# A two-layer hybrid transformer kernel: stores issued from GpSimd, attention loads for two heads at once, and other weave ratios

## The chip, the cores and the metric

The kernel runs on one core of one Trainium2 chip. A core has five engines that work side by side, each with its own instruction stream: PE (TensorE, matrix products), DVE (VectorE), ACT (ScalarE), POOL (GpSimd) and SP (SyncE, which here only issues transfers). Transfers between the device's memory and the core's on-chip memory (DMA) are issued by SP, ACT or POOL; an issue stands in the engine's stream like any other instruction, and what comes behind it waits for it. The metric is the device time of one execution, in microseconds.

## The reference

The input is 2048 latent tokens of width 1024, with 256 context tokens in front (18 tiles of 128 tokens in all). Layer 0 is "even", layer 1 is "odd". Cut to what matters:

```python
# each layer: h = rms_norm(x) * (1 + scale) + shift, for latent and context; x = x + gate * y
# layer 0 (even)
u = h @ w_in                       # q_lat, kv_lat, k_rope, za, gq, gk, gv, gate ranks, zb
q, k, v = mla_heads(q_lat, kv_lat, k_rope)       # 8 heads, 96-wide q and k, 64-wide v
a = softmax(q @ k.T * 96 ** -0.5) @ v            # every latent token sees all 2304
b = gla_bidirectional(gq, gk, gv, gates)         # 4 heads, gated scan in chunks of 64, both ways
y = concat([a * silu(za), rms_norm(b) * silu(zb)]) @ w_out
# layer 1 (odd)
q, k, v, z = split(h @ w_in, 4)                  # 16 heads, 64 wide; q and k normalised
s = q @ k_window.T / 8 + rpb                     # window of 8 rows x 16 columns on a 64-wide grid
p = softmax(concat([s, q @ k_ctx.T / 8]))
y = ((p @ concat([v_window, v_ctx])) * silu(z)) @ w_out
```

All is float32. The kernel gets products of that accuracy from three matmuls of split numbers: a factor is written as a high part and a low part, and high times high, high times low and low times high are summed.

## The kernel before

The layers run in stages, one after the other, and each leaves its results in device memory:

- `even_latent`: layer 0's latent projections, which give the queries `QT`, the keys `KT` and the values `Vn` (with high and low parts).
- `even_rest` (L540): the other projections of layer 0. Cells (tile t, column group j) of 24 matmuls each (8 steps of 3) give za (`zaT`) and the inputs of the gated scan (`Un`, in pieces of 352 or 512 columns). Woven between them are `maxes()`: for each of the 8 heads the largest score of every query row, 82 matmuls `mx` and as many reductions on DVE (L592), then one transpose (L597) and a store of the negated row `mr` into row 96 of `QT`. Attention later gets the shift of its exponential from that row.
- `even_mix` (L916): `even_attention` (L784), interleaved with the gated scan `gla` (L605), then `project` (L975) with the output weights. While it projects, `ahead()` prepares layer 1: it splits weights and prepares two token tiles (`prep`: load `x`, normalise, transpose at L299, store `H`).
- `odd_qk` (L1012): layer 1's queries and keys (`Q`, `K`), and two first cells of the values.
- `odd_vz` (L1088): the rest of the values (`V1c` for context, `V1` for latent tokens) and the gate z. Its `maxes()` goes over 16 heads: products of queries and keys, a table `mtab` that POOL makes for each head with two additions (L1134, L1135), maxima on DVE (L1151, L1162), a transpose (L1169), and four small stores `M`.
- `odd_attention` (L1181): pairs of heads j = 0 to 7, scores at L1244 and L1245, then the output projection.

In attention, scores `st` are three matmuls per key tile `kt` and head (L889, L890, L892), then an exponential on ACT, the product with the values (`av`, L865) and running sums on DVE and POOL. `keys`, `low`, `values` and `queries` issue the loads, all from SP: `akh` (high key parts with the row 96), `akl` (low parts), `av` (values), `aqh` and `aql` (queries). The first pair of heads loads in two halves; later pairs are loaded ahead while the pair before runs.

`weave(main, side, ratio, lag)` (L128) sets how two streams mix: after each step of `main` it adds `ratio` to a count and takes as many steps of `side` as the count has whole numbers. `lag` keeps `main` from being issued ahead of the side step that lies that many steps back. What is left of `side` comes at the end.

The order of instructions on each engine is fixed when the program is built: a scheduler places them by its own estimate of their times, and `issue_after` forbids it to place one before another. Waits between engines go over semaphores. Transfers issued by SP and ACT share eight DMA semaphores in turn, and a transfer waits until the one before it on its semaphore has landed; those issued by POOL have eight others. Buffers in on-chip memory come from pools; `bufs` is the number of buffers of a name, and memory of a closed pool is reused as soon as its last users are done.

Stores leave from these queues: `zaT`, `Un` of 352 columns, the maxima's rows, `V1c`, `V1` and `M` from ACT; `Un` of 512 columns from SP (two from POOL); `Q`, `K`, `QT`, `KT` from SP. Raw weights (`wraw`, L343) go through two buffers, and are split on ACT and DVE (L346).

The central lines of the weave and of its uses are

```python
due += ratio
while due >= 1:
    due -= 1
    r = next(side, None)
...
self.weave(gemms, maxes(), 1.0, 30)     # even_rest
self.weave(gemms, maxes(), 0.5, 15)     # odd_vz
```

## Time and profile before

| | us |
|---|---|
| median of 3 runs | 3861.09 (3860.72 to 3863.76) |
| the profiled execution | 3867.9 |
| its span, first to last instruction | 3866.1 |
| PE busy in it | 3670.2 |
| DVE busy | 2347.1 |
| ACT busy | 1475.4 |
| POOL busy | 1269.1 |

The mean clock granted to PE in this execution is 0.972 of full speed. Stages by the times of their first and last instructions: `even_rest` some 566 to 1124, scores of the even attention from 1124 to 2062 with the scan between them, `odd_vz` some 2715 to 3191, `odd_attention` from there on.

How rows are read. A timeline row gives start, duration, engine, line, operation, output and inputs with their sizes (partitions x elements), and in brackets the idle time of the engine before it with what ended that; a `q` behind an engine's name (SPq) is its issuing of transfers. A row of waits gives total, number and longest. A row of windows gives the stretch, its length, then for PE, PEld (loading of weights), DVE, ACT and POOL the busy time with the number of instructions, and last the granted clock, the share of the DMA engines' time and the GB/s. A row of a line gives durations in ns (least, median, largest) and first and last start.

### The profile page before, as it was taken

Reading aid. Unit: us, or ns where it says so; the run is one execution under the profiler, and the core shown is the slowest. Engines: PE = TensorE matmul, PEld = TensorE weight load, DVE = VectorE, ACT = ScalarE, POOL = GpSimd, SP = SyncE. Lnnn points to the kernel's source line nnn. Section 1 sums busy time; section 2 is a strip of 40 time slices with the busy share of each in tenths; the row PEclk is TensorE's granted clock in tenths of the full one; section 3 lists DMA queues with packets and bytes.
Section 4 is the critical chain, followed back from the end, with each engine's and each line's share of the span. In section 5 each row is a group of like instructions: output and inputs, shape, how many; then the busy total and the mean of one; then the engine's idle time right before and its main releaser. Section 6 shows DMA issues by size and latency. Waiting matters only on the chain. (4 is left out here: it accounts for less than half of the span.)

```text
span 3866.1 us, 52721 instructions
## 1 busy us (share of the span) xinstructions
PE 3670.2 (95%) x18388; PEld 2767.7 (72%) x18388; DVE 2347.1 (61%) x4699; ACT 1475.4 (38%) x2928; POOL 1269.1 (33%) x1356
## 2 busy tenths in 40 slices
PE   7999979999979999999999999999999997889899
PEld 4999878888866666555556788888788874555577
DVE  4677757888855556586654344444677765667632
ACT  3555541111115555545553123333322225656610
POOL 0334320000004444454543223333222215667622
PEclk8999989999989999999999999999999998999999
DMA  6455553222241232323514544445544468797553
GB/s 236 138 152 148 155 166 90 75 85 77 69 130 59 75 99 75 90 86 111 148 57 136 164 142 126 131 128 154 176 135 132 138 136 207 182 204 183 146 150 114
DMA packets 387175, 503.09 MB, mean 130 GB/s; under 512 B 30691, under 2 KB 265611, under 8 KB 380424
## 3 DMA queue, kind: packets, MB, share of 16 engines
q1 hardware_dynamic: 339174, 447.83, 41.1%
q10 hardware_dynamic: 47576, 51.37, 4.2%
q8 instruction: 146, 2.39, 0.3%
q14 instruction: 119, 0.97, 0.1%
q0 software_dynamic: 160, 0.52, 0.0%
HBM read 329.68 MB, written 169.93 MB: 129 GB/s over the span
## 5 line engine op out<-in xcount | busy, mean ns | idle before, releaser
L106 ACT ACTIVATE apt<-st 128x512 f32<-128x512 f32 (+1 forms) x592 | 346.1, 592 | 340.7 <-PE st L892 306.3
L592 DVE TENSOR_REDUCE mm<-mx 128x1 f32<-128x512 f32 (+1 forms) x656 | 393.2, 628 | 102.8 <-PE mx L591 95.5
L880 DVE TENSOR_TENSOR acc<-acc,apt 128x512 f32<-128x512 f32 x288 | 253.9, 903 | 174.9 <-ACT apt L106 173.4
L865 PE MATMUL av<-apt,av 128*64 128x512 f32 (+1 forms) x1184 | 306.9, 605 | 0.0
L880 POOL TENSOR_TENSOR acc<-acc,apt 128x512 f32<-128x512 f32 x160 | 216.4, 1366 | 238.6 <-ACT apt L106 237.9
L1291 POOL TENSOR_TENSOR oacc<-oacc,opt 128x341 f32<-128x341 f32 (+6 forms) x336 | 237.4, 738 | 116.5 <-ACT opt L106 92.9
L889 PE MATMUL st<-aqh,akh 97*128 97x512 f32 (+1 forms) x592 | 264.0, 446 | 11.1 <-ACT apt L106 5.8
L591 PE MATMUL mx<-mk,mq 96*128 96x512 f32 (+1 forms) x656 | 239.7, 375 | 9.4 <-DMA mq<-QT 8.5
L1162 DVE CUSTOM_DVE_ANT_1 mx<-mx,mtab 128x225 f32<-128x225 f32 (+13 forms) x576 | 180.8, 341 | 103.5 <-PE mx L1156 56.3
L890 PE MATMUL st<-aql,akh 96*128 96x512 f32 (+1 forms) x592 | 236.0, 399 | 1.2 <-DMA aql<-QT 1.2
L892 PE MATMUL st<-aqh,akl 96*128 96x512 f32 (+1 forms) x592 | 234.7, 397 | 0.0
L889 PEld LDWEIGHTS st<-aqh,akh 97*128 97x128 f32 x592 | 112.7, 191 | 137.9 <-issue 76.5
L106 ACT ACTIVATE u<-gm 128x352 f32<-128x352 f32 (+1 forms) x140 | 69.0, 498 | 357.8 <-PE gm L125 283.8
L1351 DVE TENSOR_TENSOR opt<-st,tab 128x64 f32<-128x64 f32 (+10 forms) x576 | 145.1, 313 | 73.1 <-PE st L1245 51.3
L570 POOL DMA_DIRECT2D Un<-u x2 | 1.4, 676 | 565.6 <-DVE u L559 565.6
L998 POOL TENSOR_TENSOR px<-py,px 128x512 f32<-128x512 f32 x68 | 91.2, 1343 | 283.9 <-DVE py L997 277.2
L865 PEld LDWEIGHTS av<-apt,av 128*64 128x64 f32 x1184 | 76.9, 137 | 143.3 <-issue 139.9
L997 DVE TENSOR_TENSOR py<-pj,gate 128x512 f32<-128x512 f32 x68 | 46.9, 690 | 218.0 <-PE pj L116 217.9
L1134 POOL TENSOR_TENSOR mtab<-mtab,maskq 128x1798 f32<-128x1798 f32 x16 | 51.4, 3212 | 325.0 <-DMA mtab<-rpb_q 251.1
L106 ACT ACTIVATE opt<-opt 128x465 f32<-128x465 f32 (+7 forms) x256 | 122.6, 497 | 53.6 <-DVE opt L1351 47.2
L1244 PE MATMUL st<-q,kt 128*128 128x480 f32 (+5 forms) x256 | 101.0, 406 | 39.1 <-ACT opt L106 20.9
L591 PEld LDWEIGHTS mx<-mk,mq 96*128 96x128 f32 x656 | 122.1, 189 | 22.2 <-issue 8.8
(419 smaller groups left out, 10301.7 us busy)
## 6 DMA issues: line engine op xcount, KB each, us to landing
q<-Q SPq DMA_DIRECT2D x48, 512.0 KB
kb<-K SPq DMA_DIRECT2D x192, 128.0 KB
H<-x ACTq DMA_DIRECT2D x36, 512.0 KB
pr<-RT SPq DMA_DIRECT2D x34, 512.0 KB
adaw<-ada_w SPq DMA_DIRECT2D x64, 256.0 KB
x<-H SPq DMA_DIRECT2D x32, 512.0 KB
wraw<-w_od SPq DMA_DIRECT2D x64, 256.0 KB
mtab<-rpb_q SPq DMA_DIRECT2D x16, 899.0 KB
```

The lines of the kernel that those rows point to most:

```text
L106: return self.nc.scalar.activation(out, in_, func, **kw)
L591: mm = nc.tensor.matmul(ps[:, :w], q[:A_QK, (t % 6) * P : (t % 6) * P + P], k[:A_QK, k0 : k0 + w], start=True, stop=True)
L592: nc.vector.tensor_reduce(out=m[:, t, n : n + 1], in_=ps[:, :w], axis=AX.X, op=ALU.max)
L865: nc.tensor.matmul(av[i * 64 : i * 64 + 64, :w], V[:, kt, i * 64 : i * 64 + 64], pts[i][:, :w], start=n == 0, stop=n == len(kts) - 1)
L880: eng.tensor_tensor(out=acc[i][e][:, :w], in0=a[:, :w], in1=pts[i][:, :w], op=ALU.add)
L889: nc.tensor.matmul(ps[:, :w], kh[: A_QK + 1, ks], qh[: A_QK + 1, :w], start=True, stop=False)
L890: nc.tensor.matmul(ps[:, :w], kh[:A_QK, ks], ql[:A_QK, :w], start=False, stop=False)
L892: mm = nc.tensor.matmul(ps[:, :w], kl[:A_QK, kq : kq + P], qh[:A_QK, :w], start=False, stop=True)
L1162: nc.vector.tensor_tensor_reduce(out=s, in0=s, in1=tb[:, ri : ri + rn, ci : ci + cn], scale=1.0, scalar=-3e38, op0=ALU.add, op1=ALU.max, a ...
L1244: nc.tensor.matmul(ps, k1, q1, start=True, stop=False)
L1291: eng.tensor_tensor(out=a, in0=a, in1=pts[i][:, a0 - r0 : a1 - r0, :], op=ALU.add)
L1351: nc.vector.tensor_tensor(out=pt[:, d[0], d[1]], in0=ps[:, d[0], d[1]], in1=tabs[i][:, ri : ri + rn, ci : ci + cn], op=ALU.add)
```

## The change

The diff does these things:

- `weave` gets `head`: a negative start of the count, so that the side stream begins `head` steps later. Once the side stream is at its end, each step that it would have taken is counted in `over`, and the bound on the main stream moves on by that many side steps.
- `even_rest` weaves with ratio 1.06 and head 20 in place of 1.0; `odd_vz` with 0.57 in place of 0.5.
- The stores `zaT`, all of `Un`, the maxima's rows into `QT`, `V1c`, `V1` and `M` are issued by POOL. In the built program ACT has 208 transfers fewer, SP has 110 instructions fewer, and POOL has 224 transfers more; DVE's and PE's instructions are the same in number.
- `even_attention` loads keys, low parts and queries of both heads of a pair in one transfer each, into tiles with a head dimension. The first pair comes in pieces of 384, 768 and 1152 columns. The second block's queries are issued after the first pieces, before the others. The next pair's keys are loaded in block 2 (both heads) and its values in block 4; before, it was one head each in blocks 2 and 3.
- `ahead()` yields once more behind each `prep`, so that the next one comes a project tile later.
- Raw weights of layer 1 have three buffers in place of two.
- `odd_attention` loads the first pair's values after the tables.

```diff
@@ -125,15 +125,17 @@
             yield
-    def weave(self, main, side, ratio, lag):
-        due, done = 0.0, []
+    def weave(self, main, side, ratio, lag, head=0):
+        due, done, over = -float(head * ratio), [], 0.0
         while True:
             with ExitStack() as es:
-                if len(done) > lag:
-                    es.enter_context(self.tc.issue_after(done[-lag - 1].ins))
+                n = len(done) - lag - 1 + int(over)
+                if n >= 0:
+                    es.enter_context(self.tc.issue_after(done[min(n, len(done) - 1)].ins))
                 if next(main, self) is self:
@@ -141,7 +143,9 @@
                 r = next(side, None)
-                if r is not None:
+                if r is None:
+                    over += 1
+                else:
                     done.append(r)
@@ -278,9 +282,9 @@
             nc.sync.dma_start(self.gates[l, :, (b - 4) * 512 : (b - 4) * 512 + 512], row[:])
-    def prep_pool(self, es, name, side, bufs):
+    def prep_pool(self, es, name, side, bufs, wbufs):
         self.prp = self.pool(es, name, bufs=2, side=side, reuse_waits="tile")
-        self.hbufs = bufs
+        self.hbufs, self.wbufs = bufs, wbufs
     def prep(self, l, t, src, pp, tag):
@@ -331,7 +335,7 @@
         nc = self.nc
-        sp, bufs, width = stage or (self.prp, 2, cols)
+        sp, bufs, width = stage or (self.prp, self.wbufs, cols)
         if place is None:
@@ -565,11 +569,11 @@
                     self.act(z[:], pt[:])
-                    nc.scalar.dma_start(self.zaT[:, :, t * P : t * P + P].rearrange("j p t -> p j t"), z[:])
+                    nc.gpsimd.dma_start(self.zaT[:, :, t * P : t * P + P].rearrange("j p t -> p j t"), z[:])
                 elif j == 1:
-                    (nc.gpsimd if t < 2 else nc.sync).dma_start(self.Un[t, :, 1056:], u[:])
+                    nc.gpsimd.dma_start(self.Un[t, :, 1056:], u[:])
                 else:
-                    nc.scalar.dma_start(self.Un[t, :, (j - 2) * 352 : (j - 1) * 352], u[:, :352])
+                    nc.gpsimd.dma_start(self.Un[t, :, (j - 2) * 352 : (j - 1) * 352], u[:, :352])
             cells = self.cells(list(range(NT))[::-1], (2, 3, 4, 0, 1), lambda t, j: j not in (2, 3) or t < NT - 2)
@@ -597,10 +601,10 @@
                     self.act(r[:NT], ps[:NT, :P], AF.Copy, scale=-1.0)
-                    nc.scalar.dma_start(self.QT[h, 0, A_QK].rearrange("(t p) -> t p", p=P), r[:NT].bitcast(F32))
+                    nc.gpsimd.dma_start(self.QT[h, 0, A_QK].rearrange("(t p) -> t p", p=P), r[:NT].bitcast(F32))
                     yield mm
-            self.weave(gemms, maxes(), 1.0, 30)
+            self.weave(gemms, maxes(), 1.06, 30, 20)
     def gla(self, gp, gs, g1, gd, pp, tag):
@@ -785,75 +789,70 @@
         half = T // 2
-        def keys(j, i):
-            kh = self.tl(ap, [P, T], f"akh{i}", F32R, bufs=2)
-            src = self.KT[2 * j + i, 0]
-            cuts = (0, half, T) if j == 0 else (0, T)
+        firsts = (0, 3 * P, half)
+        def keys(j):
+            kh = self.tl(ap, [P, 2, T], "akh", F32R, bufs=2)
+            cuts = firsts + (T,) if j == 0 else (0, T)
             for a, b in zip(cuts, cuts[1:]):
-                nc.sync.dma_start(kh[:A_QK, a:b].bitcast(F32), src[:A_QK, a:b])
-                nc.sync.dma_start(kh[A_QK : A_QK + 1, a:b].bitcast(F32), src[A_QK : A_QK + 1, a:b])
-                if b < T:
-                    yield kh
-            yield kh
+                nc.sync.dma_start(kh[:A_QK, :, a:b].bitcast(F32), self.KT[2 * j : 2 * j + 2, 0, :A_QK, a:b].rearrange("h p t -> p h t"))
+                nc.sync.dma_start(kh[A_QK : A_QK + 1, :, a:b].bitcast(F32),
+                                  self.KT[2 * j : 2 * j + 2, 0, A_QK : A_QK + 1, a:b].rearrange("h p t -> p h t"))
+                yield kh
         def values(j):
             V = self.tl(ap, [P, NT, P], "av", bufs=2)
-            cuts = (0, NT // 2, NT) if j == 0 else (0, NT)
+            cuts = [c // P for c in firsts + (T,)] if j == 0 else (0, NT)
             for a, b in zip(cuts, cuts[1:]):
...
         def low(j, p):
-            kl = [self.tl(ap, [P, half], f"akl{p}{i}", F32R, bufs=1) for i in range(2)]
-            for i in range(2):
-                nc.sync.dma_start(kl[i][:A_QK].bitcast(F32), self.KT[2 * j + i, 1, :A_QK, p * half : (p + 1) * half])
-            return kl
+            kl = self.tl(ap, [P, 2, half], f"akl{p}", F32R, bufs=1)
+            cuts = firsts if j + p == 0 else (0, half)
+            for a, b in zip(cuts, cuts[1:]):
+                nc.sync.dma_start(kl[:A_QK, :, a:b].bitcast(F32),
+                                  self.KT[2 * j : 2 * j + 2, 1, :A_QK, p * half + a : p * half + b].rearrange("h p t -> p h t"))
+                yield kl
         def queries(j, q0, w):
-            Q = []
-            for i, h in enumerate((2 * j, 2 * j + 1)):
-                qh = self.tl(ap, [P, 512], f"aqh{i}", F32R, bufs=2)
-                ql = self.tl(ap, [P, 512], f"aql{i}", F32R, bufs=2)
-                nc.sync.dma_start(qh[:A_QK, :w].bitcast(F32), self.QT[h, 0, :A_QK, q0 : q0 + w])
-                nc.sync.dma_start(qh[A_QK : A_QK + 1, :w].bitcast(F32), self.QT[h, 0, A_QK : A_QK + 1, q0 : q0 + w])
-                last = nc.sync.dma_start(ql[:A_QK, :w].bitcast(F32), self.QT[h, 1, :A_QK, q0 : q0 + w])
-                Q.append((qh, ql))
-            return Q, last
-        nextK, nextV = [None, None], None
+            q = self.tl(ap, [P, 4, 512], "aq", F32R, bufs=2)
+            nc.sync.dma_start(q[:A_QK, :, :w].bitcast(F32), self.QT[2 * j : 2 * j + 2, :, :A_QK, q0 : q0 + w].rearrange("h z p t -> p (h z) t"))
+            return q, nc.sync.dma_start(q[A_QK : A_QK + 1, 0::2, :w].bitcast(F32),
+                                        self.QT[2 * j : 2 * j + 2, 0, A_QK : A_QK + 1, q0 : q0 + w].rearrange("h p t -> p h t"))
+        nextK = nextV = None
+        early = {}
         for j in range(4):
-            rest = []
             if j == 0:
-                Q, _ = queries(0, 0, CTX)
-                gens = [keys(0, i) for i in range(2)] + [values(0)]
-                K = [next(g) for g in gens[:2]]
-                L = [low(0, 0)]
-                V = next(gens[2])
-                rest = gens
+                early[0], _ = queries(0, 0, CTX)
+                gens = [keys(0), low(0, 0), values(0)]
+                K, L0, V = [next(g) for g in gens]
+                early[1], _ = queries(0, CTX, 512)
+                for g in gens:
+                    next(g)
+                next(gens[0])
+                L = [L0, next(low(0, 1))]
+                next(gens[2])
             else:
-                K = list(nextK)
-                V = nextV
-                L = [low(j, 0), low(j, 1)]
+                K, V = nextK, nextV
+                L = [next(low(j, p)) for p in range(2)]
             for nb, (q0, w, kts) in enumerate(blocks):
-                if j or nb:
+                if j == 0 and nb in early:
+                    Q = early.pop(nb)
+                else:
                     Q, last = queries(j, q0, w)
...
                 nc.sync.dma_start(zt[:, :w], self.zaT[j, :, q0 : q0 + w])
-                if j < 3 and nb > 1:
+                if j < 3 and nb in (2, 4):
                     with self.tc.issue_after(last.ins):
-                        if nb < 4:
-                            nextK[nb - 2], = keys(j + 1, nb - 2)
+                        if nb == 2:
+                            nextK, = keys(j + 1)
                         else:
...
                 yield
-                if rest:
-                    for g in rest[:2]:
-                        next(g)
-                    L.append(low(0, 1))
-                    next(rest[2])
-                    rest = []
                 av = self.tl(pp, [P, 512], "av", bufs=2)
@@ -883,13 +882,12 @@
                     for i in range(2):
-                        kh = K[i]
-                        qh, ql = Q[i]
+                        qh, ql = Q[:, 2 * i, :], Q[:, 2 * i + 1, :]
                         ps = self.tl(pp, [P, 512], "st", bufs=3)
-                        nc.tensor.matmul(ps[:, :w], kh[: A_QK + 1, ks], qh[: A_QK + 1, :w], start=True, stop=False)
-                        nc.tensor.matmul(ps[:, :w], kh[:A_QK, ks], ql[:A_QK, :w], start=False, stop=False)
-                        kl, kq = L[kt // (NT // 2)][i], (kt % (NT // 2)) * P
-                        mm = nc.tensor.matmul(ps[:, :w], kl[:A_QK, kq : kq + P], qh[:A_QK, :w], start=False, stop=True)
+                        nc.tensor.matmul(ps[:, :w], K[: A_QK + 1, i, ks], qh[: A_QK + 1, :w], start=True, stop=False)
+                        nc.tensor.matmul(ps[:, :w], K[:A_QK, i, ks], ql[:A_QK, :w], start=False, stop=False)
+                        kl, kq = L[kt // (NT // 2)], (kt % (NT // 2)) * P
+                        mm = nc.tensor.matmul(ps[:, :w], kl[:A_QK, i, kq : kq + P], qh[:A_QK, :w], start=False, stop=True)
                         pt = self.tl(ap, [P, 512], "apt", bufs=8)
@@ -950,7 +948,7 @@
             pp = self.pool(es, "woP", bufs=2, space=PSUM, reuse_waits="tile")
-            self.prep_pool(e1, "prp1", "left", 2)
+            self.prep_pool(e1, "prp1", "left", 2, 3)
             ws = [self.pool(e1, "owS", side="left", reuse_waits="tile")]
@@ -958,6 +956,7 @@
                     hT[t] = self.prep(1, t, self.x1, pp, ("pj", 4))
+                    yield
                     yield
@@ -1079,11 +1078,11 @@
         if t < NCT:
-            self.nc.scalar.dma_start(self.V1c[:, t, c], v[:])
+            self.nc.gpsimd.dma_start(self.V1c[:, t, c], v[:])
             return
...
         for r in range(2):
-            self.nc.scalar.dma_start(self.V1[a + r, g * 64 : g * 64 + 64, c], v[r * 64 : r * 64 + 64])
+            self.nc.gpsimd.dma_start(self.V1[a + r, g * 64 : g * 64 + 64, c], v[r * 64 : r * 64 + 64])
     def odd_vz(self, ws, win, hT):
@@ -1170,12 +1169,12 @@
                     for g in range(4):
-                        nc.scalar.dma_start(self.M1[h, g * 512 : g * 512 + 512].rearrange("(a c b) -> c a b", a=8, c=4),
+                        nc.gpsimd.dma_start(self.M1[h, g * 512 : g * 512 + 512].rearrange("(a c b) -> c a b", a=8, c=4),
                                             r[4 * g : 4 * g + 4].rearrange("c (a b) -> c a b", a=8).bitcast(F32))
...
             gemms = self.stream(cells, hT, cell, lambda t: self.reload(1, t))
-            self.weave(gemms, maxes(), 0.5, 15)
+            self.weave(gemms, maxes(), 0.57, 15)
     def odd_attention(self, ld, right, wout):
@@ -1249,15 +1248,18 @@
                 kc = keys(j, 0, CTX, "kc")
-                V = values(j)
                 if j == 0:
...
                         pass
+                else:
+                    V = values(j)
                 if mk is None:
...
                 tabs = [table(2 * j + i, i) for i in range(2)]
+                if j == 0:
+                    V = values(j)
                 O, acc = {}, {}
@@ -1388,7 +1390,7 @@
         with ExitStack() as e0:
-            self.prep_pool(e0, "prp0", "right", 2)
+            self.prep_pool(e0, "prp0", "right", 2, 2)
             ws = self.pool(e0, "ewS", side="left", reuse_waits="tile")
```

## The prediction

> **What bounds the kernel now.** I read the summary of the engines first, then what PE's idle time waited for, then the span in short windows, and last the timeline around each hole.
>
> ```profile
> span 3866.1 us, 52721 instructions
> PE 3670.2 (95%) x18388; PEld 2767.7 (72%) x18388; DVE 2347.1 (61%) x4699; ACT 1475.4 (38%) x2928; POOL 1269.1 (33%) x1356
> ...
> PE st L1244 <- ACT opt L106: 23.8, 19, 3.5
> ...
> PE gm L123 <- ACT onat L106: 7.0, 1, 7.0
> ```
>
> PE, the matmul engine, is busy 95% of the span, so only 195.9 us (3866.1 − 3670.2) are idle. The changed program, as built, holds the same matmuls, only in another order. The time can therefore fall only by PE's idle time and by the slow clock that follows it; no engine's saving counts as such. The largest entry (L1244 on ACT, 19 short waits inside layer 1's attention) belongs to work that the change leaves alone. The rest of what it can reach sits in seams between stages. Two are large: even projections to even attention, and odd projections to odd attention.
>
> ```profile
> 1110.00:1160.00 50.00, 29.53 (x104) 19.92 (x103) 16.17 (x30) 12.12 (x24) 4.88 (x10) 0.69 0.77 204
> 3180.00:3220.00 40.00, 18.29 (x53) 11.02 (x53) 15.86 (x54) 8.52 (x16) 7.11 (x3) 0.58 1.01 210
> ```
>
> In each row the first number after the length is PE's busy time; the last three are granted clock, DMA share and GB/s. PE idles 20.5 us (50 − 29.53) from 1110 to 1160 and 21.7 us from 3180 to 3220, and what runs there runs at a mean clock of 0.69 and 0.58. Those two holes are most of what this change can win.
>
> **Step B, the first row maximum of the even weave (edit: head=20).**
>
> ```profile
> 566.33 0.32 PE L125 MATMUL gm<-W2h,hlo 128*128 128x352 f32 x1
> 566.49 0.32 PE L123 MATMUL gm<-W2h,hhi 128*128 128x352 f32 x1
> ...
> 581.62 2.04 PE L591 MATMUL mx<-mk,mq 96*128 96x256 f32 x5 [8.53 <-DMA mq<-QT]
> ```
>
> PE reaches its first maximum after 43 projection matmuls and waits 8.53 us for the queries' load. In the changed program 63 such matmuls stand ahead of it, 20 more: 352-column ones are 0.16 us apart (566.33 to 566.49), 512-column ones 0.24 (1116.62 to 1116.86, below). 15 of them are of the wide kind, so 5 × 0.16 + 15 × 0.24 = 4.4 us of the wait is filled. The load itself is no earlier: it waits for stores that the change doesn't touch. Bounds 3.2 us (all narrow) to 6; I take 4.
>
> **Step C, into the even attention (lead and ratio 1.06, two heads per load, pieces, stores off ACT).**
>
> ```profile
> 1116.62 0.40 PE L123 MATMUL gm<-wr1h,hhi 128*128 128x512 f32 x1
> 1116.86 0.39 PE L124 MATMUL gm<-wr1l,hhi 128*128 128x512 f32 x1
> 1117.32 2.88 PE L591 MATMUL mx<-mk,mq 96*128 96x512 f32 x8
> ...
> 1124.21 0.38 PE L597 MATMUL mx<-ident,mc 128*18 128x128 f32 x1 [2.52 <-DVE mc L595]
> ...
> 1136.27 0.76 PE L889 MATMUL st<-aqh,akh 97*128 97x512 f32 x1 [5.24 <-DMA aqh<-QT]
> 1147.37 0.45 PE L641 MATMUL gl<-ident,gu 128*96 128x128 f32 x1 [10.34 <-POOL gu L640]
> 1149.03 0.79 PE L890 MATMUL st<-aql,akh 96*128 96x512 f32 x1 [1.22 <-DMA aql<-QT]
> ...
> 1105.30 0.30 SPq L795 DMA_DIRECT2D akh<-KT  x1
> 1113.37 0.22 SPq L796 DMA_DIRECT2D akh<-KT  x1
> 1131.56 0.30 SPq L819 DMA_DIRECT2D aqh<-QT  x1
> 1136.69 1.24 SPq L636 DMA_DIRECT2D gu<-Un  x2
> ```
>
> The last projection is issued before 1117.32; then come left-over maxima, a few scores, and holes of 5.24 and 10.34 us. Even flow returns at 1149.03. In these 31.7 us (timeline rows not all shown) stand 10 maxima, 25 score, value and sum matmuls and two transposes, some 6 us at full clock, so 26 are lost. Three things make the loss. First, the maxima end after the projections: in the changed program their last transpose stands 39 matmuls (9 us) before the last projection. Second, SP is late: between its loads at 1105.30 and 1113.37 it stood 8.1 us. In the program that is a wait on a DMA semaphore which SP's loads share with ACT's stores; with the stores on POOL it goes, and the loads wait only for the buffers of the projections whose weights lie there: the queries' and first keys' buffers are free 42 us or more before the end, the first values' 12 to 15 us before. Third, the second block's queries (1131.56) and the gating inputs (1136.69) stand at the end of SP's queue. Now these queries are issued ahead of the later pieces, and the first gating transpose stands some 17 us of score and value work into the attention instead of behind one score matmul. What is late next: that transpose again (its load is still behind some 5 MB of keys and values; the 204 GB/s of this window move them in 25 us, from 12 to 15 us before the projections' end, so 0 to 4 us of wait remain), and the keys' third piece. The saving is 26 less 2 for the gating wait and 3 for a slower clock at the start: 21; I take 20. Bounds: 10, if the transfers set the pace (rival 1), and 26.
>
> **Step E, project and prepare (one more yield).**
>
> ```profile
> 2180.91 0.32 SPq L290 DMA_DIRECT2D x<-x  x1
> 2188.40 1.97 PE L299 MATMUL pj<-ident,x 128*128 128x128 f32 x8 [4.87 <-DVE x L296]
> 2190.59 0.63 PE L115 MATMUL pj<-gu,prh 128*128 128x512 f32 x1
> 2191.01 0.63 PE L116 MATMUL pj<-gu,prl 128*128 128x512 f32 x1
> ```
>
> PE's transposes of the second tile wait 4.87 us for x, whose load leaves at 2180.91, when the single buffer is free. With the extra yield one project tile of 48 matmuls (11 us at 0.24) stands before them, more than the wait. The matmuls after it took 0.42 us each (2190.59 to 2191.01) instead of 0.24, for some 3 us: 1.3 more. I take 6; bounds 0 (x is later too) and 7.
>
> **Step G, into the second odd weave (three raw-weight buffers).** Before PE's 7.0 us wait for `onat`, ACT stands behind two weight casts that wait for their loads and a V store. The store goes, but three casts now stand there; a load's pace with three buffers is 2/3 of the time, so 3 × 2/3 equals the 2 of before. I take 2; bounds −4 and 7.
>
> **Step H, into the odd attention (ratio 0.57, values last, V and M stores on POOL).**
>
> ```profile
> 3185.77 0.50 PE L1149 MATMUL mx<-mk,mz 128*128 128x256 f32 x2 [3.68 <-ACT mz L106]
> 3191.13 0.37 PE L1169 MATMUL mx<-ident,mc 128*16 128x128 f32 x1 [2.68 <-DVE mc L1167]
> 3195.86 1.19 PE L1244 MATMUL st<-q,kc 128*128 128x512 f32 x2 [4.36 <-DMA q<-Q]
> ...
> 3207.53 1.62 PE L1244 MATMUL st<-q,kc 128*128 128x512 f32 x3 [8.13 <-DMA q<-Q]
> 3214.75 0.44 PE L1244 MATMUL st<-q,kt 128*128 128x288 f32 x1
> ...
> 3178.37 0.48 SPq L1143 DMA_DIRECT2D mq<-Q  x1
> ...
> 3191.84 6.89 ACTq L1173 DMA_DIRECT2D M<-mr  x4
> ```
>
> Behind the last projection PE waits 3.68 us for a query load that SP issued at 3178.37 among eight value loads, 2.68 for the last maximum, 4.36 and 8.13 for queries of layer 1's attention. From 3182.1 to 3214.75 stand eight maxima and 16 score matmuls, some 5 us of work: 27.6 lost. By the changed order the last maximum's transpose stands 136 matmuls (32 us) before the last projection, so the first and second wait vanish, and so does the ACT queue's 6.89 us of M stores ahead of its exponentials. But the DMA share was 1.01 in this seam: keys, queries, tables and values must still come through it, and SP's queue now has the next pair's queries, the tables and the value loads ahead of the first keys, and among them loads of V1c, whose last store can be issued only 11 us before the last projection ends. So first scores come 6 to 8 us after that end, and the next pair of heads is again load-bound. I take 13 of the 27.6: the vanished 6.4 and about half of the 12.5 for queries. Bounds 3 and 26.
>
> **What the moved stores cost POOL.** 224 issues more (94 in the even weave, 132 in the odd one, less two that were there).
>
> ```profile
> L570 POOL DMA_DIRECT2D Un<-u x2: 556/676/797, 1112.6 to 1120.5; - x2
> ...
> DMA to landing us min/median/max: 2.6/5.3/7.9
> ...
> L1133 SPq DMA_DIRECT2D mtab<-rpb_q x16: 332/339/579, 2727.3 to 3137.0; - x16
> L1134 POOL TENSOR_TENSOR mtab<-mtab,maskq x16: 3209/3212/3216, 2735.0 to 3141.7; 128x1798 f32<-128x1798 f32 x16
> L1135 POOL TENSOR_TENSOR mtab<-mtab,maskq x16: 3710/3728/4176, 2741.8 to 3145.0; 128x1798 f32<-128x1798 f32 x16
> L1167 DVE TENSOR_REDUCE mc<-mm x15: 236/236/239, 2775.5 to 3164.7; 128x16 f32<-128x80 f32 x15
> ...
> 700.00:800.00 100.00, 99.80 (x517) 87.89 (x516) 81.75 (x139) 12.94 (x23) 0.00 (x0) 1.00 0.28 81
> 2800.00:2900.00 100.00, 100.00 (x492) 83.99 (x491) 69.63 (x305) 24.27 (x42) 27.74 (x8) 1.00 0.44 135
> ```
>
> An issue on POOL took 0.68 us. In the even weave POOL is idle (0.00 us busy from 700 to 800) and its four u buffers give each store several cells of time: nothing. In the odd weave POOL also makes each head's table: load 4.7 us (3137.0 to 3141.7) and additions of 3.2 and 3.7, together 11.7 us behind the free buffer. A head takes 27.8 us (14 intervals from 2775.5 to 3164.7), of which 16 / 0.5 × 3 × 0.23 = 22 are projections; with 0.57 it takes 25.1. Eight store issues per head are 5.4 us, so 8 us of slack remain: nothing, unless an issue costs over (25.1 − 11.7) / 8 = 1.7 us. DVE's 82% of the even weave becomes at most 87% with ratio 1.06, and 70% in the odd one 80%: still below PE, no cost.
>
> The Trainium skill speaks against these moves. In "DMA: Bandwidth & Descriptors", section "SWDGE vs HWDGE vs iDMA", it says that GpSimd writes its descriptors into SBUF, from which VectorE locks it out in two-port mode, and that transfers issued from SyncE or ScalarE are immune. No row here shows a store issued under such a lock; POOL's 16 additions took 3.209 to 3.216 us while DVE was busy 70% of the time, which shows no lock on those.
>
> **The sum.** 4 + 20 + 6 + 2 + 13 = 45 us. Against the profiled execution, 3867.9 us (span and 1.8 around it), that is 3823; the execution lies 6.8 above the median of 3861.1, so 3816 in terms of the median.
>
> **Rivals.**
> 1. Transfers set the pace at both seams: C gives 10 and H 3, with the rest 4 + 10 + 6 + 2 + 3 = 25, so 3836. For it: DMA shares of 0.77 and 1.01, with PE idle. Against it: the buffers come free 9 to 42 us earlier, while PE still has projections to do.
> 2. Both seams close: 4 + 26 + 7 + 7 + 26 = 70, so 3791. For it: everything the first scores need is written long before. Against it: V1c and the gating load.
> 3. Slower: POOL's store issues go forward only while DVE is idle, 0.68 / (1 − 0.70) = 2.3 us each. Eight are 18.1 us, and with 11.7 make 29.8 against a head's 25.1. The next table is then 4.7 us late per head, DVE's maxima wait for it, PE for their PSUM buffers: 14 × 4.7 = 66 us lost. H is lost as well, since V and M land late, and 32 us of B, C, E and G remain: 3861 + 66 − 32 = 3895. It decides from 1.7 us per issue. The skill's rule above names a mechanism of this kind. Against it: the even 3.21 us of the additions and the 0.56 to 0.80 us of the two issues.
> 4. The change moves the waits without shortening them: the gating load and V1c take the place of what goes, and the time stays within 5 us of 3861. Against it: waits of over 20 us have no successor of that length that I can name.
>
> **How the numbers follow.** Forecast 0.46, rival 1 0.24, rival 2 0.12, rival 3 0.10, rival 4 0.08. A difference of 0.2% (8 us) is about what a measurement of this kernel can tell from none. Rival 4 I split 0.02 faster, 0.04 the same, 0.02 slower. So faster 0.84, same 0.04, slower 0.12. Predicted: 3816. The forecast alone spans 3800 to 3832 (C and H together ±16). The range takes in rival 1 with some of its bounds, and most of rival 2: 3786 to 3850; left out are rivals 3 and 4 (0.18).
>
> **What would show it.** B: the first L591 wait is 4 us. C: no projection-free gap over 5 us between the last L125 and L890, and maxima ended before it. E: no wait at L299. G: a wait of 5 to 7 us at the first L123 after the V cells remains. H: no wait on `mz`, the first L1244 6 to 8 us behind the last projection. POOL: issues of 0.6 to 0.8 us, table additions ahead of need. It would be wrong if PE showed waits inside the weaves, which had none, or if a POOL issue took 2 us.

## The result and the profile after

The changed kernel took 3829.45 us (median of 4 runs, 3824.43 to 3833.95), against 3860.9 for the kernel before on the same chip: a ratio of 0.9912 [0.9898, 0.9926], 31.5 us less. Taken again later, beside three of the experiments (`base_after` below), it took 3834.55 (6 runs, 3825.0 to 3843.18), a ratio of 0.9928 [0.9914, 0.9942]. The forecast was 3816. So it is faster, as predicted, but by 28 to 31 us in place of 45.

The head of the page, and the rows of what PE waited for (total, number, longest), of the changed kernel:

```profile
span 3832.2 us, 52724 instructions
...
PE 3668.3 (96%) x18388; PEld 2759.5 (72%) x18388; DVE 2357.4 (62%) x4699; ACT 1475.2 (38%) x2928; POOL 1402.2 (37%) x1580
```

```profile
PE st L1243 <- DMA q<-Q: 13.2, 1, 13.2
...
PE gm L123 <- ACT onat L106: 7.1, 1, 7.1
...
PE mx L1168 <- DVE mc L1166: 4.5, 9, 1.0
...
PE mx L595 <- DMA mq<-QT: 3.4, 1, 3.4
```

(Lines have moved by the edit: L595 was L591, L303 L299, L1243 and L1244 were L1244 and L1245.) PE's busy time is as before, 3668.3 for 3670.2; its idle time fell from 195.9 us to 163.9 (3832.2 − 3668.3). The first maximum waits 3.4 us in place of 8.53. L303 has no entry for a `pj` transpose any more. The wait on `onat` is still there with 7.1, and the waits on layer 1's queries, once 4.36 and 8.13, are now one of 13.2. New are nine short waits at L1168, inside the odd weave, where the kernel before has a single one of 2.68 behind the last projection.

The two seams by windows (columns as in the prediction's):

```profile
1110.00:1160.00 50.00, 46.58 (x201) 28.70 (x200) 18.43 (x26) 24.64 (x45) 17.68 (x19) 1.00 0.77 201
3160.00:3190.00 30.00, 15.64 (x56) 10.51 (x57) 4.66 (x7) 6.85 (x14) 4.20 (x4) 0.72 0.90 232
3150.00:3160.00 10.00, 10.00 (x47) 8.27 (x46) 0.00 (x0) 1.65 (x3) 0.56 (x1) 1.00 1.13 219
3160.00:3170.00 10.00, 5.00 (x22) 3.76 (x21) 0.00 (x0) 0.74 (x2) 1.08 (x2) 0.91 1.03 302
```

The even seam is full: 46.58 of 50 us busy at full clock, where it was 29.53 at 0.69. The odd one still has a hole, 15.64 of 30, with the DMA engines' share above 1 ahead of it.

The even seam by PE's and SP's timelines:

```profile
1117.03 0.39 PE L125 MATMUL gm<-wr1h,hlo 128*128 128x512 f32 x1
1117.27 0.28 PE L887 MATMUL st<-aq,akh 97*128 97x256 f32 x1
...
1119.86 0.38 PE L887 MATMUL st<-aq,akh 97*128 97x256 f32 x1 [1.36 <-ACT apt L106]
...
1141.06 0.31 PE L645 MATMUL gl<-ident,gu 128*96 128x128 f32 x1
```

```profile
1067.32 0.32 SPq L822 DMA_DIRECT2D aq<-QT  x1
1067.74 0.68 SPq L823 DMA_DIRECT2D aq<-QT  x1
...
1105.58 0.52 SPq L822 DMA_DIRECT2D aq<-QT  x1
...
1128.83 1.51 SPq L640 DMA_DIRECT2D gu<-Un  x2
```

The first score follows the last projection by 0.24 us, the longest gap is 1.36, and the first gating transpose (L645) at 1141.06 waits for nothing. SP issues the second of the two loads of the first queries (1067.74) right behind the first; the second block's queries leave at 1105.58, 26 us earlier than before, and the gating input at 1128.83.

The odd seam, by PE, SP and POOL, with the landing times of the `V1c` stores:

```profile
3164.62 0.39 PE L125 MATMUL gm<-w1h,hlo 128*128 128x512 f32 x1
3178.16 1.19 PE L1243 MATMUL st<-q,kc 128*128 128x512 f32 x2 [13.15 <-DMA q<-Q]
```

```profile
3153.89 0.84 SPq L1238 DMA_DIRECT2D tab<-rpb_k  x2
3164.75 1.23 SPq L1231 DMA_DIRECT2D ov<-V1c  x2
...
3167.22 1.15 SPq L1215 DMA_DIRECT2D kc<-K  x2
...
3170.03 1.71 SPq L1203 DMA_DIRECT2D q<-Q  x2
```

```profile
3156.32 0.56 POOL L1081 DMA_DIRECT2D V1c<-ovz  x1 [6.70 <-ACT ovz L106]
...
DMA to landing us min/median/max: 4.6/7.5/11.1
```

Here SP stood from 3154.73 (3153.89 + 0.84) to 3164.75 in front of the `V1c` load (L1231). The store for which it waited left POOL at 3156.32 and landed at 3164.69 in the trace; the `V1c` stores took 4.6 to 11.1 us to land. The first keys (L1215) come behind it, at 3167.22, with the end of the projections already past.

### The profile page after: what moved, and what is told of

It is laid out like the page before. It is cut to its first block, busy times and chain, and to the rows that moved or that the text cites. A ratio compares the mean times of both kernels' runs of the same rounds, so it can differ in the third digit from the quotient of the medians.

```text
span 3832.2 us, 52724 instructions
## 1 busy us (share of the span) xinstructions
PE 3668.3 (96%) x18388; PEld 2759.5 (72%) x18388; DVE 2357.4 (62%) x4699; ACT 1475.2 (38%) x2928; POOL 1402.2 (37%) x1580
## 5 line engine op out<-in xcount | busy, mean ns | idle before, releaser
L1293 POOL TENSOR_TENSOR oacc<-oacc,opt 128x341 f32<-128x341 f32 (+7 forms) x336 | 237.2, 738 | 110.6 <-ACT opt L106 82.7
L887 PE MATMUL st<-aq,akh 97*128 97x512 f32 (+1 forms) x592 | 264.3, 447 | 5.2 <-ACT apt L106 5.0
L595 PE MATMUL mx<-mk,mq 96*128 96x512 f32 (+1 forms) x656 | 237.1, 374 | 5.6 <-DMA mq<-QT 3.4
L888 PE MATMUL st<-aq,akh 96*128 96x512 f32 (+1 forms) x592 | 235.6, 398 | 0.0
L890 PE MATMUL st<-aq,akl 96*128 96x512 f32 (+1 forms) x592 | 234.6, 397 | 0.0
L887 PEld LDWEIGHTS st<-aq,akh 97*128 97x128 f32 x592 | 112.6, 190 | 137.6 <-issue 89.8
L1243 PE MATMUL st<-q,kt 128*128 128x480 f32 (+5 forms) x256 | 101.8, 408 | 39.1 <-ACT opt L106 20.3
L890 PEld LDWEIGHTS st<-aq,akl 96*128 96x128 f32 x592 | 113.6, 192 | 31.2 <-issue 5.7
L595 PEld LDWEIGHTS mx<-mk,mq 96*128 96x128 f32 x656 | 121.9, 189 | 17.2 <-DMA mk<-KT 3.8
L106 ACT ACTIVATE prh<-pr 128x1024 fp32r<-128x1024 f32 x34 | 35.7, 1056 | 252.1 <-PE pj L115 252.1
```

Source lines behind the costliest of these rows:

```text
L106: return self.nc.scalar.activation(out, in_, func, **kw)
L595: mm = nc.tensor.matmul(ps[:, :w], q[:A_QK, (t % 6) * P : (t % 6) * P + P], k[:A_QK, k0 : k0 + w], start=True, stop=True)
L887: nc.tensor.matmul(ps[:, :w], K[: A_QK + 1, i, ks], qh[: A_QK + 1, :w], start=True, stop=False)
L888: nc.tensor.matmul(ps[:, :w], K[:A_QK, i, ks], ql[:A_QK, :w], start=False, stop=False)
L890: mm = nc.tensor.matmul(ps[:, :w], kl[:A_QK, i, kq : kq + P], qh[:A_QK, :w], start=False, stop=True)
L1243: nc.tensor.matmul(ps, k1, q1, start=True, stop=False)
```

## The experiments

The stages are compared by the start times of matmuls in each trace. (a) goes from the last projection of `even_rest` to the last score of the even attention, (b) from there to the last matmul of `project`, (c) from the first odd maximum to the first score of a latent key tile (`kt`) in the odd attention, (d) from the same start to the last product with values (`o`), (e) from that to the last matmul. For example (a) of the kernel before is 2062.6 − 1117.1 = 945.5, and of the changed one 2043.7 − 1117.0 = 926.7. The part between (b) and (c), with the first cells of the values, lasted 460 to 463.5 us in all fourteen traces.

| kernel | median us | ratio [95%] | a | b | c | d | e |
|---|---|---|---|---|---|---|---|
| before | 3861.1 | 1 | 945.5 | 216.1 | 473.4 | 929.8 | 188.8 |
| changed | 3829.45 | 0.9912 [0.9898, 0.9926] | 926.7 | 211.5 | 468.3 | 919.4 | 188.5 |
| `base_after` (changed, again) | 3834.55 | 0.9928 [0.9914, 0.9942] | 928.1 | 212.2 | 468.4 | 925.2 | 189.5 |
| `u_stores` | 3835.1 | 0.9936 [0.9918, 0.9954] | 930.9 | 211.1 | 472.6 | 918.6 | 189.1 |
| `u_weave` | 3840.58 | 0.9942 [0.9926, 0.9957] | 931.4 | 212.4 | 469.8 | 920.2 | 189.2 |
| `u_loads` | 3843.81 | 0.9955 [0.9941, 0.9970] | 943.8 | 208.6 | 468.4 | 916.7 | 188.1 |
| `u_yield` | 3839.0 | 0.9942 [0.9926, 0.9958] | 927.5 | 217.4 | 469.1 | 921.4 | 189.4 |
| `u_wbufs` | 3836.77 | 0.9934 [0.9921, 0.9948] | 924.6 | 209.5 | 476.3 | 921.5 | 188.8 |
| `u_odd` | 3843.34 | 0.9947 [0.9934, 0.9961] | 923.8 | 211.7 | 467.3 | 921.2 | 195.3 |
| `f_v1c` | 3834.59 | 0.9929 [0.9914, 0.9944] | 923.9 | 212.3 | 465.2 | 913.9 | 192.3 |
| `f_order` | 3834.09 | 0.9926 [0.9912, 0.9939] | 923.3 | 211.9 | 456.2 | 917.6 | 195.6 |
| `f_hold` | 3830.06 | 0.9917 [0.9905, 0.9930] | 923.9 | 212.2 | 457.1 | 919.7 | 187.9 |
| `p_stores` | 3862.35 | 1.0001 [0.9992, 1.0010] | 937.9 | 216.4 | 470.6 | 927.4 | 196.0 |
| `p_loads` | 3845.31 | 0.9955 [0.9940, 0.9969] | 934.5 | 216.8 | 474.7 | 929.0 | 190.2 |

What an edit cannot reach shows the scatter of one trace: (a) lies between 923.3 and 928.1 in the changed kernel and those of its variants whose edits lie behind it, (d) between 916.7 and 925.2 in the changed kernel and the variants that differ in layer 0 alone. Single runs of one kernel lie up to 18 us apart (`base_after`: 3825.0 to 3843.18). So differences of some 5 us are read from the stage and the row that they belong to, not from the medians. Nor is the traced run always near its median: it lies 8 us below in `f_v1c` and 7 below in `u_odd`, 9 above in `base_after` and 11 above in `p_loads`. Names with `u_` undo one part in the changed kernel, with `f_` change it further, with `p_` put one part alone into the kernel before.

**`u_stores`: all stores back to ACT and SP.**

```diff
-                    nc.gpsimd.dma_start(self.Un[t, :, (j - 2) * 352 : (j - 1) * 352], u[:, :352])
+                    nc.scalar.dma_start(self.Un[t, :, (j - 2) * 352 : (j - 1) * 352], u[:, :352])
...
```

> The changed kernel with all moved stores back on their old queues (ACT, and SP for the 512-column Un); weaves, loads and buffers as changed. Theory: the stores matter through SP, whose loads share DMA semaphores with ACT's stores; SP stands for about 8 us again ahead of the first keys, of which the earlier end of the maxima hides part, and M and V1c stores queue on ACT again before the odd attention. About 4 us are lost at the even seam and 4 at the odd one: 3829 + 8 = 3837. Rival 1: the weaves and the loads do all of it, and the stores nothing: 3825 to 3833. Rival 2: the stores are what closed the seams: 3850 or more, with PE waiting over 8 us between the last even projection and the even flow of the attention.

Timelines of this kernel: SP's two loads of the first queries, ACT's store between them, and then ACT and PE behind the seam:

```profile
1067.12 0.33 SPq L822 DMA_DIRECT2D aq<-QT  x1
1072.69 0.68 SPq L823 DMA_DIRECT2D aq<-QT  x1
```

```profile
1070.83 0.33 ACTq L576 DMA_DIRECT2D Un<-u  x1
```

```profile
1139.51 0.63 ACT L106 ACTIVATE gw<-ge 97x512 fp32r<-97x512 f32 x1 [8.11 <-DMA ge<-gate_w]
...
1140.67 0.79 PE L887 MATMUL st<-aq,akh 97*128 97x512 f32 x1 [5.81 <-ACT apt L106]
```

SP stands again, 5.2 us between two loads that write one tile (1067.12 + 0.33 to 1072.69), so for no buffer. In the trace the second load uses the same DMA semaphore as the `Un` store that ACT issues at 1070.83, and it leaves 1.86 us after that store. What it costs shows 26 us behind the last projection: ACT waits 8.11 us for the gating weights `ge`, which come late in SP's queue (ACT takes them up 25.1 us behind the last projection, in the changed kernel 20.1). Its exponentials stand behind that, and PE waits 5.81 us for them; in the changed kernel the two waits are 3.06 and 0.77. (a) is 3 to 4 us longer, (c) 4, and the wait on layer 1's queries 16.9 in place of 13.2. So the wait of SP's loads on ACT's stores is real, and is worth some 4 us at each seam while the other edits are in place; at the odd seam nothing of it is left in (d).

**`u_weave`: the even weave as before.**

```diff
-            self.weave(gemms, maxes(), 1.06, 30, 20)
+            self.weave(gemms, maxes(), 1.0, 30)
```

> The changed kernel with the even weave as before (ratio 1.0, no head). Theory: the 8.5 us wait at the first maximum comes back (+4 to 5), and ten maxima with their reductions and the transpose stand behind the last projection again (+3 to 6 of waits, since the scores can only start behind them): 3829 + 9 = 3838. Rival: the loads of the attention are on time without the lead, the scores fill in for the late maxima, and only the first wait comes back: 3833 or 3834.

The first maximum waited 7.8 us, 4.4 more than the 3.4 of the changed kernel, and (a) grew by 3.3 to 4.7, with a wait of 3.1 us for the last head's maxima in it (another of 1.9 stands in the weave). Step B's 4 us at the first maximum is borne out, and the left-over maxima cost some 4 more.

**`u_loads`: the even attention's loads as before, one head each, halves.**

```diff
-            kh = self.tl(ap, [P, 2, T], "akh", F32R, bufs=2)
-            cuts = firsts + (T,) if j == 0 else (0, T)
+            kh = self.tl(ap, [P, T], f"akh{i}", F32R, bufs=2)
+            cuts = (0, half, T) if j == 0 else (0, T)
...
```

> The changed kernel with the loads of the even attention as before (one head each, halves, the second block's queries last). Theory: the hole of 5.2 us for the second block's queries comes back, and a part of the 10.3 us for the gating inputs behind them, with a slow clock: 3829 + 12 = 3841. Rival: with the stores off ACT and the maxima done early SP runs through the old loads in time, and nothing comes back: 3826 to 3833.

PE's timeline at the even seam:

```profile
1128.25 0.45 PE L645 MATMUL gl<-ident,gu 128*96 128x128 f32 x1 [9.28 <-POOL gu L644]
...
1135.08 0.76 PE L651 MATMUL gl<-gw,rT 98*128 98x512 f32 x1 [6.38 <-DMA aqh<-QT]
```

The holes are back, 9.28 us for the gating input and 6.38 for the second block's queries, and (a) is 16 to 17 us longer. Of the edits at the even seam this one weighs most.

**`f_v1c`: the first two pairs' loads of `V1c` behind the first keys.**

```diff
-                nc.sync.dma_start(V[:, :NCT, :], self.V1c[:, :, c])
+                with ExitStack() as ev:
+                    if j < 2:
+                        ev.enter_context(self.tc.issue_after(lastkb.ins))
+                    nc.sync.dma_start(V[:, :NCT, :], self.V1c[:, :, c])
```

> The changed kernel with the loads of the first two pairs' context values (from V1c) held back until the first pair's keys are issued. In the changed kernel SP stands 10 us for the last V1c store, with the first keys and queries of the odd attention behind it. Theory: that wait is the hole of 13.2 us ahead of the first scores; without it the first scores come within 5 us of the last projection, and the time falls by 8 to 10 us: 3820. Rival: the transfers set the pace there (DMA share 1.02 to 1.13 from 3150 to 3180); the first scores come at most 3 us earlier, and the time stays at 3826 to 3830.

The wait for the first queries fell from 13.2 us to 9.5 only, though the first keys now left SP 8.7 us ahead of the last projection (3150.24 and 3158.89) in place of 2.6 behind it. So the `V1c` load was a part of the wait; the rest fell only when loads of pair 1 were held back as well (`f_order` and `f_hold`). The total did not move, where 3820 was expected.

**`f_order`: besides, everything that pair 1 loads, behind the first keys of pair 0.**

```diff
+                with ExitStack() as eh:
+                    if j == 1:
+                        eh.enter_context(self.tc.issue_after(lastkb.ins))
+                    Q = queries(j)
...
```

> As the kernel before this one (V1c held back), and the second pair's queries, tables and values too are held back until the first pair's keys and queries are issued. In f_v1c the wait for the first queries fell only from 13.2 to 9.5 us, with a DMA share of 1.01 to 1.22 in the 25 us before: transfers set the pace, but among them are 1.5 MB of queries and 1 MB of tables for the second pair, which is needed some 55 us later. Theory: what sets the pace is their place in the queue; without them (2.5 MB at 0.2 to 0.27 MB/us is 9 to 12 us) the first queries land as the last projection ends: a wait of at most 3 us, and 8 to 10 us less than the changed kernel, 3820. Rival: the DMA engines are simply full with the first pair's own loads and the last stores; the wait stays at 7 to 10 us and the time at 3827 to 3833; or the second pair is late later and gives it back in the attention.

PE's and POOL's timelines:

```profile
3161.40 0.71 PE L1246 MATMUL st<-q,kc 128*128 128x512 f32 x2 [1.53 <-ACT ovz L106]
...
3276.02 1.97 PE L777 MATMUL st<-oacc,mtwos 128*64 128x512 f32 x2 [8.13 <-POOL oacc L1300]
```

```profile
3267.42 4.69 POOL L1242 TENSOR_TENSOR tab<-tab,maskk 128x1034 f32<-128x1034 f32 x2 [9.16 <-DMA tab<-rpb_k]
```

The seam is closed, with a wait of 1.53 in place of 13.15, and (c) is 12 us shorter. Yet (d) is within the scatter of the changed kernel's: POOL waited 9.16 us for pair 2's tables, its sums `oacc` for pair 1 stood behind them, and PE stood 8.13 us for these.

**`u_odd`: the odd weave at 0.5.**

```diff
-            self.weave(gemms, maxes(), 0.57, 15)
+            self.weave(gemms, maxes(), 0.5, 15)
```

> The changed kernel with ratio 0.5 in the odd weave. Theory: 0.57 gains little: it takes away the waits of 3.7 and 2.7 us behind the last projection, but costs about 5 us of short waits inside the weave (transposes of maxima waiting for DVE, 4.5 us in 9 places), and the first queries come no earlier, since transfers hold them: 3827 to 3833. Rival: the maxima's early end is what the odd seam needed; with 0.5 both waits come back and the seam opens by 8 us or more: 3837 and up.

PE's timeline at the odd seam, and its last large wait:

```profile
3155.49 0.37 PE L1168 MATMUL mx<-ident,mc 128*16 128x128 f32 x1 [2.90 <-DVE mc L1166]
3160.74 1.19 PE L1243 MATMUL st<-q,kc 128*128 128x512 f32 x2 [4.88 <-DMA q<-Q]
...
3172.65 1.62 PE L1243 MATMUL st<-q,kc 128*128 128x512 f32 x3 [8.29 <-DMA q<-Q]
...
3646.87 0.79 PE L114 MATMUL pj<-wo0h,prh 128*128 128x512 f32 x1 [10.33 <-DVE rl L782]
```

The waits of the kernel before are back at the seam (2.90, 4.88, 8.29), and (c) is the same, 467.3 for 468.3. From the last projection to the first `kt` score it takes 30.6 us in place of 21.4, but the weave ahead of it, from the first maximum to the last projection, takes 436.6 in place of 446.9: ratio 0.57 moves some 10 us from behind the last projection to before it, and in (c) of these traces it gains nothing. The median is 9 us above that of `base_after`, and the trace cannot say why, since it is of the fastest of the four runs (3835.96). In it (e) is 6 to 7 longer, with a wait of 10.33 us at the first matmul of the output projection, but `f_order`, which has ratio 0.57, shows that wait too. So what the ratio brings in the total stays open.

**`u_yield`: without the second yield in `ahead()`.**

```diff
                     yield
-                    yield
```

> The changed kernel without the extra yield between the two prepared tiles. Theory: the wait of 4.9 us for the second tile's x comes back with about 1 us of slow clock: 3829 + 5 = 3834, and the stretch from the last score of the even attention to the end of its projection is 216 us again in place of 211.5. Rival: with three raw-weight buffers that load leaves earlier anyway: 3829, and the stretch stays below 213.

```profile
2171.38 1.93 PE L303 MATMUL pj<-ident,x 128*128 128x128 f32 x8 [4.76 <-DVE x L300]
```

The wait for x is back with 4.76 us, and (b) is 5 to 6 us longer.

**`u_wbufs`: two buffers of raw weights.**

```diff
-            self.prep_pool(e1, "prp1", "left", 2, 3)
+            self.prep_pool(e1, "prp1", "left", 2, 2)
```

> The changed kernel with two raw-weight buffers for layer 1 as before. Theory: the third buffer gains nothing: the wait of 7 us for the last value cells into the odd weave is there with two and with three buffers: 3826 to 3832. Rival: with two buffers the casts fall behind and the wait grows by 3 us or more: 3833 and up.

PE's timeline, inside the odd weave:

```profile
2729.72 1.12 PE L1114 MATMUL tp<-ident,ovz 128*128 128x128 f32 x4 [2.99 <-DVE ovz L1111]
```

The wait on `onat` stayed (6.7 us with two buffers, 7.1 with three), and so did the time between (b) and (c): 461.9 for 462.4. But (c) was 8 us longer, and 7.0 of them lie in the weave: 453.9 us from the first maximum to the last projection, against 446.8 to 447.2 in every other trace with ratio 0.57. The first odd maximum stands at 2717.5 here and at 2717.7 in the changed kernel. With two buffers ACT and DVE still split weights then: the last two splits start on ACT at 2731.20, in the changed kernel the last one at 2697.86. So DVE is late with its part of the weave, and PE waits 2.99 us behind DVE at L1114 and 2.14 at L1155. So the splits do fall behind, as the rival said, though not at the wait that it named: the third buffer is worth some 7 us in the weave, of which 2 or none are left in (d).

**`f_hold`: as `f_v1c`, and of pair 1 only the queries held back.**

```diff
+                    with ExitStack() as eq:
+                        if j == 1:
+                            eq.enter_context(self.tc.issue_after(lastkb.ins))
+                        Q = queries(j)
...
```

> As f_order, but only the second pair's queries (1.5 MB) are held back; its tables and values stay early. f_order closed the seam (the odd weave's first maximum to the first score took 448.9 us against 460.5) and gave it back: waits of 8.1 us for a sum on POOL, whose queue stood 9.2 us at the next table's load, and 11.1 us ahead of the last projection. Theory: the give-back in the attention comes from tables that are late on POOL; with tables early the seam's wait is 4 to 6 us (1 MB more ahead of the queries), the 8.1 us hole does not come, and the time is 3821 to 3828. Rival: the transfers are a debt, and what is held back at the seam is paid in the attention whichever loads it is: the stretch from the first local scores to the last output takes 458 us or more, and the time stays at 3830 to 3836.

PE's, POOL's and SP's timelines:

```profile
3162.16 0.71 PE L1246 MATMUL st<-q,kc 128*128 128x512 f32 x2 [1.60 <-DMA q<-Q]
...
3274.75 1.97 PE L777 MATMUL st<-oacc,mtwos 128*64 128x512 f32 x2 [8.43 <-POOL oacc L1301]
```

```profile
3267.37 2.36 POOL L1242 TENSOR_TENSOR tab<-tab,maskk 128x1034 f32<-128x1034 f32 x1 [10.60 <-DMA tab<-rpb_k]
```

```profile
3256.52 3.97 SPq L1236 DMA_DIRECT2D ov<-V  x5
3260.58 0.93 SPq L1241 DMA_DIRECT2D tab<-rpb_k  x2
```

The seam is closed again (1.60), and the gain is gone again, at the same place: POOL waits 10.60 us for pair 2's tables, which SP issued only at 3260.58, behind value loads. The expectation, that with pair 1's tables early the hole of 8 us would not come, failed. In the changed kernel the same addition and its load stand so (POOL, then SP):

```profile
3267.81 2.38 POOL L1239 TENSOR_TENSOR tab<-tab,maskk 128x1034 f32<-128x1034 f32 x1 [5.61 <-DMA tab<-rpb_k]
```

```profile
3262.76 0.87 SPq L1238 DMA_DIRECT2D tab<-rpb_k  x2
```

The odd weave begins 5 us later in the changed kernel's trace than in the two variants', so times are counted from the first odd maximum. Pair 2's tables then leave SP at 545.1 and are taken up by POOL at 550.1 here, at 549.8 and 554.9 in `f_order`, at 547.5 and 554.3 in `f_hold`: 2 to 5 us later in the variants, though their pair 0 began 11 to 12 us earlier. The tables' buffers did not hold that load. DVE's last reads of pair 0's tables, in whose buffers pair 2's go, in the changed kernel and in `f_hold`:

```profile
3243.81 2.21 DVE L1353 TENSOR_TENSOR opt<-st,tab 128x124 f32<-128x124 f32 x12
```

```profile
3233.34 2.21 DVE L1361 TENSOR_TENSOR opt<-st,tab 128x124 f32<-128x124 f32 x12
```

They ended 17 us before the load left (3246.02 to 3262.76) in the changed kernel, and 25 us before it (3235.55 to 3260.58) in `f_hold`. What is left is what SP issues ahead of it, the value loads above all; no run issued these tables earlier. Nor is a plain limit of the transfers excluded, the rival that was on record for `f_hold`: the DMA engines' share lies between 0.74 and 1.04 in every 20 us from 3200 to 3300 in these three traces, and the stretch from the first `kt` score to the last product with values took 462.6 us, where that rival said 458 or more. The starts of the pairs (first `kt` score, us from the first odd maximum):

| kernel | pair 0 | pair 1 | pair 2 | pair 3 |
|---|---|---|---|---|
| before | 473.4 | 527.6 | 586.1 | 643.7 |
| changed | 468.3 | 518.7 | 578.0 | 635.9 |
| `f_order` | 456.2 | 510.9 | 578.0 | 635.5 |
| `f_hold` | 457.1 | 512.8 | 575.5 | 635.3 |

From pair 2 to pair 3 each of these takes 57 to 60 us. The 11 to 12 us that the two variants win at the seam are 6 to 8 at pair 1, 0 to 2.5 at pair 2 and 0.5 at pair 3.

**`p_stores` and `p_loads`: the stores alone, and the even attention's loads alone, in the kernel before.** Their diffs are those lines of the change.

> The kernel before with only the stores moved to POOL. Theory: alone they let SP run ahead by the 8 us for which it stood between the first keys' loads, but the late maxima, the second block's queries at SP's end and the gating input stay: 6 to 8 us less at the even seam, little at the odd one: 3861 - 8 = 3853. Rival 1: what SP gains is lost behind the maxima: 3858 to 3862. Rival 2, the slower side: POOL's issues delay the tables and the time rises: over 3866.

> The kernel before with only the even attention's loads changed. Theory: the second block's queries come ahead of the later pieces, so the hole of 5.2 us closes and the first gating transpose is later in the order; SP still stands for ACT's stores, and the maxima still end late. Taking the loads back cost 17 us in this stage; alone they bring a little less: 3861 - 13 = 3848. Rival: without the early end of the maxima and with SP's waits they bring half or less: 3853 and up.

The stores alone shorten (a) by 7.6 and (c) by 2.8, and the total stays (1.0001), where 3853 was expected. In the trace (e) is 7.2 us longer, by a wait of this kernel's row

```profile
PE pj L114 <- DVE rl L778: 11.0, 1, 11.0
```

where the kernel before has none on `rl`; whether the other runs have it too is not known. The loads alone shorten (a) by 11.0 and bring 0.9955. In the changed kernel the loads' undoing cost 16 to 17 and the stores' 3 to 4: the loads are worth more, and the stores less, with the other edits in place. Which of those makes the difference was not separated.

**`base_after`: the changed kernel again.**

> The changed kernel again, as the measure for the others on the same chip: 3829 within 5 us if the earlier runs were on a like chip; if it lies at 3833 to 3836, as much is to be taken off the differences of the kernels that were run later.

Its rows are those of the table; it gives the scatter by which the others are read.

## Why the prediction was right, and where it was wrong

The direction and the range were right; the sum was 14 to 17 us too large. B and C together lack 5 to 7 of their 24 us, H 3 to 8 of its 13, and E and G, at the places that they named, some 4 of their 8.

- **Step B (4 us): right.** The wait fell by 5.1 (8.53 to 3.4), the bounds of 3.2 to 6 held, and the undoing gave back 4.4.
- **Step C (20): right in its mechanisms, a few us too high.** B took the projections' end no earlier: it stood at 1117.1 and stands at 1117.0. 10 maxima (2.4 us at 0.24 each) now run ahead of it, which accounts for half of B's 5.1. So (a) shows most of B and C together: 17.4 to 18.8 us, for 24. The three causes named were each shown by an undoing: the maxima's end (`u_weave`), SP's stand (`u_stores`), the second block's queries and the gating input (`u_loads`). The seam itself closed more fully than the 5 us allowed for gating and slow clock. What fell short is in the rest of the stage: PE's idle time in (a) fell by 18 to 22 us (35.3 before, 13.3 and 17.4 in the two traces of the changed kernel), but its busy time did not fall (910.2, then 913.4 and 910.7), though the ten maxima are out of it. Why is open.
- **Step E (6): right.** (b) fell by 3.9 to 4.6, its undoing cost 5 to 6, within the bounds of 0 to 7.
- **Step G (2): wrong in its place.** At the wait for `onat` nothing came (7.0 and 7.1). The third buffer took the splitting of weights out of the odd weave instead, some 7 us by `u_wbufs`; the prediction has no term for that.
- **Step H (13): this is the term that was furthest off for its size.** (c) fell by 5.0, (d) by 4.6 to 10.4, and the third buffer is in both: without it (`u_wbufs`) (c) is 476.3, longer than the 473.4 of the kernel before, and (d) 921.5. The statement "So first scores come 6 to 8 us after that end" failed first: they came 13.5 us after it (3164.62 to 3178.16). The things that would delay them were named, the next pair's queries and tables and `V1c` in SP's queue, but priced at about half of the old 12.5 us of waits; they took all of it. `f_v1c` puts 3.6 us of the 13.2 on `V1c`, and holding the next pair's queries back as well takes 8 more (9.54 in `f_v1c`, 1.53 in `f_order`, 1.60 in `f_hold`). Second, the vanished waits on `mz` and on the last maximum were counted as 6.4 us of gain, and DVE at 80% as no cost. DVE came to 81.12% (the window below), and PE then waited 4.5 us in nine pieces at L1168, inside the weave, which the prediction had named as a sign of being wrong; in (c) the trace of `u_odd` shows the two sides to be equal. Third, and not in the prediction at all: a hole closed at this seam is not time saved. Pair 2's tables come no earlier when pair 0 starts earlier, and `f_order` and `f_hold`, which close the hole, gain nothing in (d) that stands out of its scatter.
- **POOL's issues: right.** They were to cost 0.6 to 0.8 us and hold nothing up. The groups (busy, mean ns), the line of the table additions (least, median, largest ns), and two windows of the weaves:

```profile
L1172 POOL DMA_DIRECT2D M<-mr x64 | 37.7, 596 | 91.7 <-ACT mr L106 83.1 <-issue 8.6
...
L576 POOL DMA_DIRECT2D Un<-u x50 | 27.3, 546 | 215.6 <-ACT u L106 211.3 <-issue 4.2
L572 POOL DMA_DIRECT2D zaT<-zt x18 | 13.7, 761 | 201.6 <-ACT zt L106 165.0 <-ACT mr L106 36.5
```

```profile
L1133 POOL TENSOR_TENSOR mtab<-mtab,maskq x16: 3203/3207/3221, 2708.4 to 3083.1; 128x1798 f32<-128x1798 f32 x16
```

```profile
700.00:800.00 100.00, 99.86 (x521) 88.55 (x520) 83.69 (x144) 14.52 (x26) 10.56 (x18) 1.00 0.26 82
2800.00:2900.00 100.00, 99.28 (x493) 83.15 (x492) 81.12 (x339) 26.00 (x44) 45.97 (x39) 1.00 0.43 138
```

An issue of these groups took 0.546 to 0.761 us, the first additions 3.2 as before, and PE stayed full (99.86 and 99.28 of 100).

- **Rival 1 (transfers at both seams, 3836)** is wrong at the even seam, which the loads' new order closed at the same DMA share of 0.77, and half right at the odd one: queue order and transfers kept the hole. The measured medians lie between it and the forecast. **Rival 2** is right at the even seam and wrong at the odd one; and the runs that closed both (`f_order`, `f_hold`) did not reach 3791, but 3834 and 3830. **Rival 3 (3895)** is out: no issue came near 1.7 us, with DVE busy 81 to 84% of the time. The Trainium skill ("DMA: Bandwidth & Descriptors", section "SWDGE vs HWDGE vs iDMA") says that VectorE, in its two-port mode, locks GpSimd out of the memory in which GpSimd writes its descriptors. 0.546 to 0.761 us under this load show no sign of such a lock here; how much of VectorE's work ran in that mode no row tells. **Rival 4** is out for the total, but its sentence that `V1c` takes the place of what goes is what happened at the odd seam.

Left open: what in the rest of the even attention takes back 5 us; what holds pair 2's tables; what ratio 0.57 brings in the total; how much "values last" brings by itself, which was not tried alone; and the tail. There the output projection's first matmul waits 3.7 and 5.2 us for ACT in the two traces of the changed kernel, but 8 to 11 for DVE's `rl` in `p_stores`, `u_odd`, `f_order` and `f_v1c`, so that (e) is 188 to 190 us in some kernels and 192 to 196 in others, with no edit near it. Those 4 to 7 us are as large as most effects studied here; what decides between the two was not found. No variant is faster than the changed kernel by more than its scatter: `f_hold`'s [0.9905, 0.9930] overlaps both of its intervals.

## What to carry to other kernels

When a hole between two stages is to be closed, look at what paces the second stage before counting the hole as a gain: here 12 us won at its start were gone two pairs later, where a later pair's tables had come no earlier. Put what the first operations of a stage need at the head of the issuing queue: undoing that at the even seam cost 16 to 17 us, undoing the move of the stores 3 to 4. A higher weave ratio takes work out of the tail only by putting it, with its waits, into the weave: subtract what the weave grows by (10.3 us here) from what the tail shrinks by (9.2). And an edit can pay at another place than the one it was made for, as the third buffer did: compare whole stages, not only the wait that was named.
